# One hybrid decoder layer: the factors' reloads on GpSimd's queue, matmuls in program order, and four small moves in the order of work

## The chip, the core and the metric

The kernel runs on one core of a Trainium2 chip. The metric is the device time of one execution in microseconds; three timed runs of the kernel before took 2387.79, 2386.2 and 2385.35 us, the median is 2386.2. A core has a matrix engine (TensorE, PE in the profile, with PEld for its weight loads), three engines for elementwise work (VectorE or DVE, ScalarE or ACT, GpSimd or POOL) and a sync engine (SP) which here does nothing but issue DMAs. DMAs can also be issued from ACT's and POOL's queues.

## The reference, cut to what matters

One decoder layer for 512 tokens and a model width of 2048, everything in float32:

```python
h = rms_norm(x, g_mix)                       # 512 x 2048
aq, ak, av, rq, rk, rv, rg = split(h @ w_in) # seven parts of 1024 columns
a_out = moba_attention(rot(norm(aq)), rot(norm(ak)), av)       # 8 heads of 128, causal
r_out = silu(rg) * normed(retention(rot(rq), rot(rk), rv)) * g_ret  # 8 heads
x = x + concat(a_out, r_out) @ w_o
h2 = rms_norm(x, g_ffn)
x = x + (silu(h2 @ w_gate) * (h2 @ w_up)) @ w_down             # inner width 5632
gate = sigmoid(rms_norm(x, g_ple) @ w_ple_gate + b_ple_gate)
x = x + (p @ w_ple_proj) * gate
```

## The kernel before, in words

**Precision.** Each float32 operand is held as two reduced-precision parts, high and low. `split()` makes them: a copy on ScalarE (L54) gives the high part, a subtraction on VectorE (L55) the low one. `mm3()` then does three matmuls, high by high, high by low and low by high, all recorded at line 64, the helper `matmul()`.

**Big products.** The products with w_in's value and gate columns (w_vg), w_o, gate and up (w_gu, eleven groups), w_down (three parts of the inner width, of 8, 8 and 6 chunks of factors) and the last gate (w_pl) use a scheme of seven products in place of eight for a product of 2 x 2 blocks. A `Group` goes through its products in the order 1, 5, 6, 3, 7, 2, 4 (`ORDER`), which accumulate into three pairs of PSUM banks, X, Z and Y. The left factors of the seven products (tiles `s`) are sums and differences of activation blocks, split into high and low; the right ones are made from weight tiles `raw` as they come in: `add()` sums two blocks in place (L82), `extract()` splits the result into `wh` and `wl`, `multiply()` issues the matmuls. `run()` steps through (product, unit) pairs: in step i it extracts unit i+2, adds unit i+3 and multiplies unit i, then calls what `later()` put down for that step. `evacuate()` reads the banks when a product is done and forms the four quarters of the result, each handed to a `finish()` of its own.

**Factors on their way to the next layer part.** `finish()` of a residual or swiglu group passes results through `to_factors()` and `factors()`, which transpose, make the sums for the seven products and split them. Most of them don't fit in place: `spill()` writes them in tiles `o` and stores these to DRAM through SP's queue; `reload()` (L196 to L203) brings a whole factor tile `s` of 1 to 2 MB back, also through SP's queue, once the last matmul that reads the old tile has been issued. This happens at each passage from one layer part to the next: w_o to gate and up (from 861), gate and up to w_down (from 1700), between w_down's three parts, and w_down to the last gate (up to 2224).

**What sets the order.** A planner places instructions on each engine by priority and simulated readiness, and adds the semaphore waits. It may reorder, except where `keep_in_program_order` pins an instruction. `in_order[0]` makes `matmul()` and `transpose()` pin, and is set for the attention and retention part (about 285 to 740 us) until `take_over()` clears it. Outside that stretch the planner is free to put matmuls of the next product among those of the current one. SP's queue is one list: an instruction that waits there holds all that stand behind it.

**The start.** `beside()` loads two chunks of x transposed for each step, scales each by the norm's gain on ScalarE (L450) and splits it; the program has both scalings of a step first, then both splits. Ten idle matmuls (L396) run while the first data comes. The first matmuls are of a `Plain` projection into banks Y and Z.

**Attention, retention and p.** For each pair of heads, `projection()` multiplies h by 8 units of weights; `weights()` keeps two or three units loaded and split ahead (`ready`). The work of the pair before is placed in numbered slots among the projection's matmuls, 32 to a projection, by `tick()` and `at_slot()`. `heads()` gives the slots: for each of a pair's two heads (`plans`) when the two turnings, the four scores, the four turned weights and the result go. Scores and results share two PSUM banks, `at`. After the last projection, the product of p with its weights (pTH, then four blocks `w_pp`) is run between L896 and L913; its results go to DRAM through GpSimd's queue (L910).

**The end.** `gate()` finishes the last two groups: `finish()` multiplies by the row's scale and adds the bias (L1004), then a sigmoid on ScalarE, a product with p's tile (L1006), the residual (L82) and the store. For the last product, "4", a subtraction from the bank comes before this.

Of the kernel before, what the change touches and what calls it, by code (L numbers as in the profile page):

```python
# [10 lines left out]
F32 = mybir.dt.float32  # L11
# [22 lines left out]
def layer_kernel(ctx, tc, x, xT, pT, g_mix, wqk, w_vg, qk_norm, g_ret, w_ow, g_ffn,  # L34
# [24 lines left out]
                                           op0=ALU.mult, op1=ALU.subtract)  # L59

    in_order = [False]

    def matmul(*args, **kw):
        ins = nc.tensor.matmul(*args, **kw)  # L64
        if in_order[0]:
            tc.keep_in_program_order(ins)

    def transpose(o, a):
        ins = nc.tensor.transpose(o, a, ident)  # L69
# [126 lines left out]
    def reload(tiles, where, n, wait={}):  # L196

        def go(p):
            tiles[p] = factor_tile(p)
            nc.sync.dma_start(tiles[p][:, :n].bitcast(F32), where[p][:, :n].bitcast(F32))  # L200
            if n == 4 and p == "4":
                nc.sync.dma_start(tiles[p][:, 6:].bitcast(F32), where[p][:, 4:].bitcast(F32))
        return lambda p: later(wait[p], lambda: go(p)) if p in wait else go(p)  # L203

    class Group:
# [70 lines left out]
            for u in range(len(groups[0].units)):  # L276
                groups[0].load(q, u)

    def evacuate(finish, ahead=None):

        def evac(g, p):
            X, Y, Z = (g.bank.get(k) for k in "XYZ")
            quarter = QUARTER.get(p)
            early = [ahead(*quarter, b) if quarter and ahead else None for b in range(2)]

            def go():
                if p == "1":
                    g.e1 = [ev_tile("e1") for _ in range(2)]
                elif p == "5":
                    g.e5 = [ev_tile("e5") for _ in range(2)]  # L290
                elif p == "6":
                    g.v = [ev_tile("v") for _ in range(2)]
                for b in range(2):
                    if p == "1":
                        nc.scalar.activation(g.e1[b], X[b], AF.Copy)
                    elif p == "5":
                        nc.scalar.activation(g.e5[b], Z[b], AF.Copy)
                    elif p == "6":
                        sub(g.v[b], Y[b], g.e1[b])
                    elif p == "3":  # L300
                        plus(g.v[b], Z[b], g.v[b])
                        finish(*quarter, b, g.v[b], early[b])
                    elif p == "7":
                        sub(g.e1[b], Y[b], g.e1[b])
                        plus(g.e5[b], g.e5[b], g.e1[b])
                        finish(*quarter, b, g.e5[b], early[b])
                    elif p == "2":
                        finish(*quarter, b, X[b], early[b])
                    elif p == "4":
                        sub(g.e1[b], Y[b], g.e1[b])  # L310
                        finish(*quarter, b, g.e1[b], early[b])
            later(1 if p == "5" else 2, go)
        return evac

# [20 lines left out]
    def residual(n, i, units, old, new, turn):  # L335

        outs = {}

        def ahead(th, nh, b):
            t = ev_tile("g", 4, name="xin")  # L340
            nc.sync.dma_start(t, old(2 * th + b, 2 * n + nh))
            return t

        def finish(th, nh, b, part, t):
            tb = 2 * th + b
            s = 2 * n + nh
            o = t if (th, nh) == (0, 0) else part
            plus(o, part, t)
            later(1, lambda: nc.sync.dma_start(new(tb, s), o))
            if turn is None:  # L350
                return
            j, gain, where, tiles = turn
            sq = ev_tile("A", name="sq")
            nc.scalar.activation(sq, o, AF.Square, accum_out=ssq[j][:, tb, s:s + 1])
            outs[tb, nh] = o
            if len([k for k in outs if k[1] == nh]) < NB:
                return
            for u in range(2):
                k = 4 * n + 2 * nh + u
                sink = spill(where, k)  # L360
                if n == 1:
                    direct = into(tiles, k)
                    sink = (lambda p, a=spill(where, k - 2), b=direct: a(p) if p == "4" else b(p)) if nh else direct
                wait = 1 + 2 * u if n == 0 else units - 2 + u if nh else 1 + u
                later(wait, lambda u=u, sink=sink: to_factors(
                    lambda b: outs[b, nh], 2 * u, sink, lambda c: gain[:, 4 * s + c:4 * s + c + 1]))
            if n == 1 and nh == 0:
                rstd_of(ssq[j], rstd[j])
        return evacuate(finish, ahead)

    in_units = lambda us: [(p, u) for part in us for p in "156" for u in part] + \
# [21 lines left out]
    warm = ev_tile("v", name="warm")  # L393
    nc.scalar.activation(warm[:, :P], zeros[:, :P], AF.Copy)
    idle = tp_p.tile([P, T], F32, name="tp", tag="tp")
    for _ in range(10):  # L396
        nc.tensor.matmul(idle, zeros[:, :P], zeros, start=True, stop=True)

    class Plain:
# [90 lines left out]
    def beside(i):  # L490

        if i == 3:
            for t, c in ((ident, ident_c), (gf, g_ffn), (gp, g_ple), (gr, g_ret)):
                nc.sync.dma_start(t, c)
        if -2 <= i < NC // 2 - 2:
            if i == -2:
                first.load(0)
            chunks[i + 2] = [h_chunk(k) for k in (2 * i + 4, 2 * i + 5)]
            for c, t in enumerate(chunks[i + 2]):
                split(h[:, 2 * i + 4 + c, 0, :], h[:, 2 * i + 4 + c, 1, :], t)  # L500
            if i > -2:
                first.load(i + 2)
        if 0 <= i + 1 < NC // 2:
            first_factors(i + 1, chunks.pop(i + 1))
        for at, q in ((3, "11"), (7, "12"), (11, "22")):
            if at <= i < at + 4:
                groups[0].load(q, i - at)
        if 8 <= i < 24:
            b, s = divmod(i - 8, NS)
            t = ev_tile("o", 4, name="xn")  # L510
            tc.keep_in_program_order(nc.sync.dma_start(t, x[b * P:(b + 1) * P, s * T:(s + 1) * T]))
            nc.scalar.activation(t, t, AF.Square, accum_out=ssq[0][:, b, s:s + 1])
        elif i == 24:
            rstd_of(ssq[0], rstd[0])
# [37 lines left out]
    stream = [wqk[i, u] for i in range(1, 2 * NPAIR) for u in range(NC // 2)] + [pT] + [w_pp[n] for n in range(NS)]  # L552
    ready = []

    def weights():
        while stream and len(ready) < (3 if len(stream) > NS - 1 else 2):
            tags.append(tags.pop(0))
            raw = rawq.tile([P, 2, T], F32, name="raw", tag=tags[0])
            wh = wq.tile([P, 2, T], F32R, name="wh", tag="wh")
            wl = wq.tile([P, 2, T], F32R, name="wl", tag="wl")  # L560
            nc.sync.dma_start(raw, stream.pop(0))
            split(wh, wl, raw)
            ready.append((wh, wl))
        return ready.pop(0)

    def projection(rows):

        accs = [acc_p.tile([P, T], F32, name="acc", tag="acc") for _ in range(4)]
        for u in range(NC // 2):
            wh, wl = weights()  # L570
            for f in range(4):
                tick()
                at = slice(f * P, (f + 1) * P)
                for c in range(2):
                    k = 2 * u + c
                    H, L = hT[k]
                    if rows:
                        mm3(accs[f], H[:, at], L[:, at], wh[:, c, :], wl[:, c, :], k == 0, k == NC - 1)
                    else:
                        mm3(accs[f], wh[:, c, at], wl[:, c, at], H, L, k == 0, k == NC - 1)  # L580
        return accs

    sides = ap.tile([P, 3, P], F32, name="sides", tag="dec")
# [268 lines left out]
    def heads(i, made):  # L852
# [7 lines left out]
        if i < NPAIR:  # L860
            plans = ((12, (15, 16, 19, 20), (19, 20, 23, 24), 27), (21, (25, 26, 39, 40), (29, 30, 42, 43), 46))
            if i == 0:
                plans = ((17, (20, 21, 24, 25), (24, 25, 28, 29), 33), (26, (30, 31, 39, 40), (38, 39, 43, 44), 47))
            for j, (turns, steps_s, steps_w, last) in enumerate(plans):
                turned, scores, weights_turned, result = attend(*made, v, j)
                put(turned, turns, turns + 1)
# [116 lines left out]
                                         (2, gp, s_h3, s_e) if kg == 2 else None), None, after))  # L983

    bias_t = []

    def load_bias():
        for s in range(NS):
# [4 lines left out]
    def gate(n):  # L993
        def ahead(th, nh, b):
            tb, s = 2 * th + b, 2 * n + nh
            t = [ev_tile("g", 4, name="xin"), ev_tile("g", 4, name="pp")]
            nc.sync.dma_start(t[0], xd[3][tb][:, s])
            nc.sync.dma_start(t[1], ppd[tb][:, s])
            return t

        def finish(th, nh, b, part, t):
            tb, s = 2 * th + b, 2 * n + nh
            o = ev_tile("A", name="y") if (th, nh) == (0, 0) else part
            nc.vector.scalar_tensor_tensor(o, part, rstd[2][:, tb:tb + 1], bias_t[s], op0=ALU.mult, op1=ALU.add)  # L1004
            nc.scalar.activation(o, o, AF.Sigmoid)
            nc.vector.tensor_tensor(o, o, t[1], op=ALU.mult)  # L1006
            plus(o, o, t[0])
            nc.sync.dma_start(out[tb * P:(tb + 1) * P, s * T:(s + 1) * T], o)
        return evacuate(finish, ahead)

    for n in range(2):
        groups.append(Group(lambda kh, nh, u, n=n: w_pl[n, kh, nh, u], range(4), s_e, gate(n),
# [81 lines left out]
```

## Time and profile before

| what | value |
|---|---|
| timed runs, us | 2387.79, 2386.2, 2385.35 (median 2386.2) |
| the profiled execution, its own time | 2389.06 us |
| its span | 2387.3 us |
| busy: PE, PEld, DVE, ACT, POOL | 97%, 80%, 81%, 50%, 2% |
| matmuls | 10470 |
| mean granted TensorE clock | 0.993 of full speed |
| DMA traffic | 463.60 MB, mean 194 GB/s |
| the chain that ended last | PE 79%, DVE 12%, DMA 5% |

The span lies between the first and the last instruction of the profiled execution; the time of that execution is 1.8 us longer. A busy share is the part of the span in which an engine had an instruction under way. Matmuls are pipelined: one of 512 columns shows as 0.39 to 0.50 us, and the next starts about 0.23 us after it.

### The profile page before, as it was taken

Reading aid. Unit: us, or ns where it says so; the run is one execution under the profiler, and the core shown is the slowest. Engines: PE = TensorE matmul, PEld = TensorE weight load, DVE = VectorE, ACT = ScalarE, POOL = GpSimd, SP = SyncE. Lnnn points to the kernel's source line nnn. Section 1 sums busy time; section 2 is a strip of 40 time slices with the busy share of each in tenths; the row PEclk is TensorE's granted clock in tenths of the full one; section 3 lists DMA queues with packets and bytes.
Section 4 is the critical chain, followed back from the end, with each engine's and each line's share of the span. In section 5 each row is a group of like instructions: output and inputs, shape, how many; then the busy total and the mean of one; then the engine's idle time right before and its main releaser. Section 6 shows DMA issues by size and latency. Waiting matters only on the chain.

```text
span 2387.3 us, 29151 instructions
## 1 busy us (share of the span) xinstructions
PE 2323.2 (97%) x10470; PEld 1901.7 (80%) x10470; DVE 1944.3 (81%) x2625; ACT 1204.9 (50%) x1791; POOL 48.2 (2%) x47
## 2 busy tenths in 40 slices
PE   9999999999999999999999999999999999999898
PEld 7888877778877777888888888888878878888677
DVE  8888676666667988888988898889888878789897
ACT  7644444444455565545554455455544433356543
POOL 0000021100010000000000000000000000000000
PEclk9999999999999999999999999999999999999999
DMA  6634733446666684356435643464587666867664
GB/s 230 240 129 161 233 102 119 128 139 189 188 217 257 227 311 162 122 177 187 143 117 167 198 142 126 143 199 153 198 341 232 253 242 220 324 222 249 253 203 124
DMA packets 166098, 463.60 MB, mean 194 GB/s; under 512 B 18497, under 2 KB 31169, under 8 KB 160961
## 3 DMA queue, kind: packets, MB, share of 16 engines
q1 hardware_dynamic: 161968, 453.34, 56.0%
q10 hardware_dynamic: 2704, 4.20, 0.7%
q0 software_dynamic: 1280, 4.20, 0.5%
q8 instruction: 82, 1.34, 0.2%
q14 instruction: 64, 0.52, 0.1%
HBM read 352.09 MB, written 105.38 MB: 192 GB/s over the span
## 4 chain that ended last, share of the span: by engine, by line
PE 79%; DVE 12%; DMA 5%; issue 2%; ACT 2%; POOL 0%; SPq 0%; ACTq 0%; DVEq 0%; POOLq 0%
PE Y L64 29%; PE Z L64 19%; PE X L64 17%; PE acc L64 9%; DVE wl L55 3%; DVE raw L82 3%; PE at L64 2%; DMA h<-o 2%; PE tp L69 2%; ACT wh L54 1%; DMA mix<-o 1%; DVE s L55 1%; DVE t L79 1%; DVE o L55 0%; DVE e L79 0%
## 5 line engine op out<-in xcount | busy, mean ns | idle before, releaser
L54 ACT ACTIVATE wh<-raw 128x1024 fp32r<-128x1024 f32 (+1 forms) x728 | 769.1, 1059 | 827.6 <-PE Y L64 289.2
L55 DVE TENSOR_TENSOR wl<-raw,wh 128x1024 fp32r<-128x1024 f32 (+1 forms) x728 | 883.1, 1218 | 277.2 <-ACT wh L54 276.3
L64 PE MATMUL Y<-wh,s 128*128 128x512 f32 x2160 | 680.8, 391 | 9.7 <-ACT wh L54 9.7
L64 PEld LDWEIGHTS Y<-wh,s 128*128 128x128 f32 x2160 | 405.3, 188 | 97.2 <-ACT wh L54 14.1
L64 PE MATMUL Z<-wh,s 128*128 128x512 f32 x1504 | 476.0, 392 | 2.6 <-DMA s<-h 1.6
L82 DVE TENSOR_TENSOR raw<-raw 128x1024 f32<-128x1024 f32 x376 | 453.0, 1217 | 27.4 <-DMA raw<-in_w_gu 9.6
L64 PE MATMUL Y<-wl,s 128*128 128x512 f32 x1080 | 425.1, 394 | 1.4 <-DVE wl L55 1.3
L64 PE MATMUL X<-wh,s 128*128 128x512 f32 x1312 | 416.9, 393 | 8.0 <-ACT wh L54 5.1
L64 PEld LDWEIGHTS Z<-wh,s 128*128 128x128 f32 x1504 | 282.1, 188 | 62.0 <-ACT wh L54 2.8
L64 PE MATMUL Z<-wl,s 128*128 128x512 f32 x752 | 297.1, 395 | 4.6 <-DVE wl L55 4.5
L64 PEld LDWEIGHTS X<-wh,s 128*128 128x128 f32 x1312 | 247.3, 189 | 62.1 <-ACT wh L54 7.8
L64 PE MATMUL X<-wl,s 128*128 128x512 f32 x656 | 258.7, 394 | 4.9 <-DVE wl L55 4.7
L64 PEld LDWEIGHTS Y<-wl,s 128*128 128x128 f32 x1080 | 203.2, 188 | 45.6 <-DVE wl L55 4.3
L64 PEld LDWEIGHTS Z<-wl,s 128*128 128x128 f32 x752 | 141.6, 188 | 37.9 <-DVE wl L55 9.3
L64 PE MATMUL acc<-h,wh 128*128 128x512 f32 x512 | 160.4, 394 | 0.8 <-DVE m L666 0.8
L64 PEld LDWEIGHTS X<-wl,s 128*128 128x128 f32 x656 | 124.1, 189 | 34.0 <-DVE wl L55 8.4
L64 PE MATMUL acc<-wh,h 128*128 128x512 f32 x384 | 130.8, 400 | 1.5 <-DVE m L666 1.1
L64 PEld LDWEIGHTS acc<-h,wh 128*128 128x128 f32 x512 | 92.5, 188 | 17.5 <-issue 1.2
L64 PE MATMUL acc<-h,wl 128*128 128x512 f32 x256 | 100.1, 391 | 0.0
L64 PEld LDWEIGHTS acc<-wh,h 128*128 128x128 f32 x384 | 72.9, 190 | 17.0 <-issue 2.7
L64 PE MATMUL acc<-wl,h 128*128 128x512 f32 x192 | 75.6, 394 | 0.0
L79 DVE TENSOR_TENSOR e<-Y,e 128x512 f32<-128x512 f32 x96 | 62.8, 682 | 14.5 <-PE Y L64 14.5
(193 smaller groups left out, 2069.7 us busy)
## 6 DMA issues: line engine op xcount, KB each, us to landing
raw<-in_w_gu SPq DMA_DIRECT2D x176, 512.0 KB, 4.3
raw<-in_w_dn SPq DMA_DIRECT2D x88, 512.0 KB, 6.1
a<-o SPq DMA_DIRECT2D x154, 256.0 KB, 2.6
raw<-in_wqk SPq DMA_DIRECT2D x63, 512.0 KB, 3.8
s<-a SPq DMA_DIRECT2D x14, 2048.0 KB, 10.8
raw<-in_w_vg SPq DMA_DIRECT2D x48, 512.0 KB, 5.2
raw<-in_w_ow SPq DMA_DIRECT2D x32, 512.0 KB, 6.1
xin<-x SPq DMA_DIRECT2D x64, 256.0 KB, 6.0
```

The costliest lines, as they stand in the source:

```text
L54: nc.scalar.activation(H, src, AF.Copy)
L55: nc.vector.tensor_tensor(L, src, H.bitcast(F32), op=ALU.subtract)
L64: ins = nc.tensor.matmul(*args, **kw)
L69: ins = nc.tensor.transpose(o, a, ident)
L79: nc.vector.tensor_tensor(o, a, b, op=ALU.subtract)
L82: nc.vector.tensor_tensor(o, a, b, op=ALU.add)
```

## The change

All reloads of factors are issued from GpSimd's queue. Every matmul that isn't pinned gets a dependency without a semaphore on the matmul before it in the program, so that the planner keeps their order; transposes are not in that chain. `weights()` is cut into `fill(n)` and the pop; after the last of its units, a projection with fewer than four units left in the stream calls `fill(3)`. In the first pair's plan the first head's result goes from slot 33 to 32 and the second head's second score from 31 to 33. At the start each chunk is scaled and split before the next is loaded, and 13 idle matmuls take the place of 10. For the last gate, `minus` holds the negated row scale; when product "7" is done, `ready()` turns the partial sum into bias minus scale times it, and product "4" then needs a single instruction from the bank in place of a subtraction and a scale-and-add.

```diff
+    last_mm = [None]
     def matmul(*args, **kw):
         ins = nc.tensor.matmul(*args, **kw)
         if in_order[0]:
             tc.keep_in_program_order(ins)
+        elif last_mm[0] is not None:
+            tc.add_manual_dep(ins.ins, last_mm[0], mybir.DependencyInfo(mybir.DependencyClass.NoSync, mybir.DependencyReason.DATA),
+                              reason="matmuls in program order")
+        last_mm[0] = ins.ins.name
...
         def go(p):
             tiles[p] = factor_tile(p)
-            nc.sync.dma_start(tiles[p][:, :n].bitcast(F32), where[p][:, :n].bitcast(F32))
+            nc.gpsimd.dma_start(tiles[p][:, :n].bitcast(F32), where[p][:, :n].bitcast(F32))
             if n == 4 and p == "4":
-                nc.sync.dma_start(tiles[p][:, 6:].bitcast(F32), where[p][:, 4:].bitcast(F32))
+                nc.gpsimd.dma_start(tiles[p][:, 6:].bitcast(F32), where[p][:, 4:].bitcast(F32))
...
                         finish(*quarter, b, g.e5[b], early[b])
+                        if ready is not None:
+                            ready(*QUARTER["4"], b, g.e1[b])
...
                     elif p == "4":
-                        sub(g.e1[b], Y[b], g.e1[b])
-                        finish(*quarter, b, g.e1[b], early[b])
+                        if ready is None:
+                            sub(g.e1[b], Y[b], g.e1[b])
+                        finish(*quarter, b, g.e1[b], early[b], *([Y[b]] if ready else []))
...
                 rstd_of(ssq[j], rstd[j])
+                if j == 2:
+                    nc.vector.tensor_scalar(minus, rstd[j], -1.0, None, op0=ALU.mult)
...
-    for _ in range(10):
+    for _ in range(13):
...
-            chunks[i + 2] = [h_chunk(k) for k in (2 * i + 4, 2 * i + 5)]
-            for c, t in enumerate(chunks[i + 2]):
-                split(h[:, 2 * i + 4 + c, 0, :], h[:, 2 * i + 4 + c, 1, :], t)
+            chunks[i + 2] = []
+            for k in (2 * i + 4, 2 * i + 5):
+                t = h_chunk(k)
+                split(h[:, k, 0, :], h[:, k, 1, :], t)
+                chunks[i + 2].append(t)
...
-    def weights():
-        while stream and len(ready) < (3 if len(stream) > NS - 1 else 2):
+    def fill(n):
+        while stream and len(ready) < n:
...
+    def weights():
+        fill(3 if len(stream) > NS - 1 else 2)
         return ready.pop(0)
...
+        if len(stream) < NS:
+            fill(3)
         return accs
...
-                plans = ((17, (20, 21, 24, 25), (24, 25, 28, 29), 33), (26, (30, 31, 39, 40), (38, 39, 43, 44), 47))
+                plans = ((17, (20, 21, 24, 25), (24, 25, 28, 29), 32), (26, (30, 33, 39, 40), (38, 39, 43, 44), 47))
...
+    minus = stat.tile([P, NB], F32, name="minus", bufs=1)
...
+        def ready(th, nh, b, w):
+            tb, s = 2 * th + b, 2 * n + nh
+            nc.vector.scalar_tensor_tensor(w, w, minus[:, tb:tb + 1], bias_t[s], op0=ALU.mult, op1=ALU.add)
+
-        def finish(th, nh, b, part, t):
+        def finish(th, nh, b, part, t, bank=None):
             tb, s = 2 * th + b, 2 * n + nh
             o = ev_tile("A", name="y") if (th, nh) == (0, 0) else part
-            nc.vector.scalar_tensor_tensor(o, part, rstd[2][:, tb:tb + 1], bias_t[s], op0=ALU.mult, op1=ALU.add)
+            nc.vector.scalar_tensor_tensor(o, part if bank is None else bank, rstd[2][:, tb:tb + 1],
+                                           bias_t[s] if bank is None else part, op0=ALU.mult, op1=ALU.add)
```

## Rows read from the trace of the kernel before

**Rows 1.** The page, busy time of each engine over the span.
```profile
PE 2323.2 (97%) x10470; PEld 1901.7 (80%) x10470; DVE 1944.3 (81%) x2625; ACT 1204.9 (50%) x1791; POOL 48.2 (2%) x47
```

**Rows 2.** Busy by stretch: length, PE, PEld, DVE, ACT, POOL, clock, DMA share, GB/s.
```profile
690.17:705.65 15.48, 11.80 (x51) 9.11 (x50) 15.47 (x26) 11.28 (x22) 4.53 (x8) 1.00 0.81 262
868.00:893.00 25.00, 23.36 (x109) 18.79 (x108) 19.94 (x36) 16.84 (x34) 0.00 (x0) 1.00 0.93 349
893.00:940.00 47.00, 39.64 (x159) 29.90 (x158) 41.53 (x58) 25.59 (x44) 1.01 (x1) 0.89 0.42 169
940.00:1740.00 800.00, 800.00 (x3603) 661.28 (x3603) 687.04 (x814) 408.20 (x528) 0.00 (x0) 1.00 0.51 163
1740.00:1785.00 45.00, 40.59 (x182) 32.34 (x181) 33.70 (x41) 19.41 (x26) 0.00 (x0) 1.00 0.89 361
1920.00:1940.00 20.00, 17.61 (x71) 14.07 (x70) 14.71 (x15) 5.76 (x6) 0.00 (x0) 0.91 1.02 417
2150.00:2245.00 95.00, 89.23 (x403) 70.81 (x403) 93.33 (x144) 62.09 (x116) 1.11 (x1) 1.00 0.80 285
2245.00:2256.00 11.00, 8.90 (x24) 6.47 (x23) 6.87 (x10) 4.67 (x7) 0.00 (x0) 0.70 0.18 50
```

**Rows 3.** The same view, stretches at the lower clock (columns as in rows 2).
```profile
9.07:12.48 3.41, 3.41 (x10) 2.65 (x9) 3.41 (x9) 3.41 (x9) 0.00 (x0) 0.50 1.05 408
343.58:346.99 3.41, 3.41 (x13) 2.93 (x12) 3.41 (x8) 1.01 (x2) 0.57 (x1) 0.50 0.00 0
896.54:906.77 10.23, 7.50 (x21) 5.21 (x22) 8.62 (x20) 9.40 (x20) 1.01 (x1) 0.50 1.03 415
```

**Rows 4.** Waits of SP's queue, 855 to 912: total us, times, longest.
```profile
SPq L200 <- DMA h<-o: 7.9, 2, 5.2
```

**Rows 5.** Waits of ScalarE, 855 to 905: total us, times, longest.
```profile
ACT o L54 <- DMA h<-o: 10.6, 2, 6.3
```

**Rows 6.** Timeline at the start: start, duration, instruction, [idle before <- releaser].
```profile
6.83 0.72 ACT L450 ACTIVATE x<-x,gm 128x512 f32<-128x512 f32 x1 [0.22 <-DMA x<-in_xT]
7.46 0.61 ACT L54 ACTIVATE h<-x 128x512 fp32r<-128x512 f32 x1
...
8.12 0.50 PE L64 MATMUL Y<-wh,h 128*128 128x512 f32 x1 [2.45 <-ACT h L54]
```

**Rows 7.** Timeline of TensorE, two pairs of matmuls that go first.
```profile
225.81 0.74 PE L64 MATMUL Y<-wh,s 128*128 128x512 f32 x2 [0.74 <-ACT wh L54]
...
993.73 0.71 PE L64 MATMUL Z<-wh,s 128*128 128x512 f32 x2
```

**Rows 8.** Timeline of VectorE just before the second of them.
```profile
990.83 1.22 DVE L55 TENSOR_TENSOR wl<-raw,wh 128x1024 fp32r<-128x1024 f32 x1
```

**Rows 9.** Timeline of TensorE, the first pair's result.
```profile
342.20 0.50 PE L64 MATMUL at<-PH,v 128*128 128x512 f32 x1 [2.12 <-ACT pt L719]
```

**Rows 10.** Timeline of TensorE, the waits at p's product.
```profile
696.27 0.50 PE L64 MATMUL acc<-wl,wh 128*128 128x512 f32 x1 [2.33 <-DVE wl L55]
...
703.36 0.50 PE L64 MATMUL acc<-wl,wh 128*128 128x512 f32 x1 [1.34 <-DVE wl L55]
```

**Rows 11.** The reloads' line L200: issue ns (min/median/max), landing us.
```profile
L200 SPq DMA_DIRECT2D s<-a x21: 319/326/383, 1700.0 to 2085.6; - x21
L200 SPq DMA_DIRECT2D s<-h x14: 319/320/468, 861.0 to 2224.0; - x14
...
DMA to landing us min/median/max: 5.3/9.9/13.4
```

**Rows 12.** GpSimd's stores of p, line L910: issue ns, landing us.
```profile
L910 POOL DMA_DIRECT2D pp<-pp x16: 539/540/731, 691.8 to 725.7; - x16
...
DMA to landing us min/median/max: 2.7/6.9/8.8
```

**Rows 13.** Timeline of VectorE, first and last instruction after the last matmul.
```profile
2378.18 0.69 DVE L79 TENSOR_TENSOR e<-Y,e 128x512 f32<-128x512 f32 x1 [2.96 <-PE Y L64]
...
2383.01 0.69 DVE L82 TENSOR_TENSOR e<-e,xin 128x512 f32<-128x512 f32 x1
```

More of the change, by code (lines that the diff above doesn't have):

```diff
@@ L277, in chained, with evacuate @@
                 groups[0].load(q, u)
-    def evacuate(finish, ahead=None):
+    def evacuate(finish, ahead=None, ready=None):
         def evac(g, p):
@@ L1008, in finish @@
             nc.sync.dma_start(out[tb * P:(tb + 1) * P, s * T:(s + 1) * T], o)
-        return evacuate(finish, ahead)
+        return evacuate(finish, ahead, ready)
     for n in range(2):
```

## The prediction

> **What bounds the kernel now.** The page comes first: TensorE is busy for 97% of the span, VectorE for 81%, ScalarE for half [rows 1]. A busy TensorE is therefore the ground, and only time in which it stands idle, or runs at the lower clock, can be won. The table by stretch says where that is [rows 2]. In the eleven gate-and-up groups, from 940 to 1740, PE is busy for 800.00 of 800 us: nothing is to be had there. Idle time sits where one layer part passes into the next: 868 to 940 (1.6 + 7.4 us), 1740 to 1785 (4.4), 1920 to 1940 (2.4) and 2150 to 2256 (5.8 + 2.1). In three of the four the DMA engines are full for most of the time, and in the first and last VectorE is close to full as well. Then the clock: after such idle time the granted clock falls to 0.5, the lower level of 1.2 GHz, and PE works on at half speed [rows 3]; short rows like the first two stand also at 1930.8, 2244.8 and 2251.6 (3.4 us each), and half of such a stretch's busy time is lost. The waits of the SP queue and of ScalarE tell why data is late at a passage [rows 4, 5]: the reloads of the factors (L200) stand in SP's queue until a spill store has landed, 7.9 us around 861 to 870, and everything behind them stands too, weights included; ScalarE waits 10.6 us for stores from the spill buffers that left late.
>
> **The edits, each with its sum.** The sum is made on the profiled execution, which took 2389.06 us with a span of 2387.3; that is 2.9 above the median of the three timed runs, 2386.2, from which I subtract.
>
> *Start (L396, L498).* The second chunk's scaling holds ScalarE at 6.83, after 0.22 us of waiting for its DMA, and the first split follows only at 7.46; the first matmul waits for that until 8.12 [rows 6]. Split behind scaling lets the split go at 6.61, 0.85 sooner. Three more idle matmuls (L396) cost nothing, since PE is idle then anyway for 2.45 us. If the shorter pause keeps the clock up, the half-speed row from 9.07 loses nothing, 3.41 / 2 = 1.7 more. Against that, matmuls in program order want the second chunk's low part at the fifth matmul, where now twelve others go first; three steps of the kind of that 0.61 us split lie before it, so I estimate it some 2 us late for that. From -1 to 2.6; I take 0.9.
>
> *Program order for unpinned matmuls (L63).* Now two matmuls of the next product often stand ahead of the last ten, or last 22, of the one before. There are 69 such pairs outside the pinned stretch. Five of them (at 147, 224, 825, 1866 and 2025) pull the next product's weights forward to before ScalarE has split them, and cost 0.74 us of idle and 0.9 us of pitch each, as at 225.81 [rows 7]; the matmuls passed over were ready. 5 x 0.9 = 4.5. The other pairs fill no hole: at 993.73 the pair goes first, yet the low weights of the product it overtakes were done at 990.83 + 1.22 = 992.05 [rows 7, 8]. From 0 to 6; I take 4.5.
>
> *First pair's result a slot earlier (L863).* The result's matmul waits 2.12 us at 342.20 for the exponential of a score from three slots before, since the two `at` banks are both with scores; then the clock falls, and 343.58 to 346.99 goes at half speed, 1.7 us lost [rows 3, 9]. In the new plan the result takes the free bank first, and the second score comes two slots later. It then waits for that same exponential, but two thirds of the time has been filled with the result. 3.8 less a new wait of some 0.8 is 3.0; from 0 to 3.8.
>
> *p's second weights (L555, L581).* PE waits 2.33 us at 696.27 and 1.34 at 703.36, both times for low weights from VectorE [rows 10]. The fill at the end of the last projection brings the first of the two splits ahead of the rotary work, so the first wait goes. But VectorE is busy for 15.47 of the 15.48 us from 690 to 705.6 [rows 2], and what is late next is the third block's split at its end: it moves up only by the one subtraction (1.2 us) that left the queue. So 1.2, from 0 to 3.7.
>
> *Reloads on GpSimd's queue (L200, L202).* Thirty-five reloads of 1 to 2 MB and two small ones leave SP; each issue cost SP 0.32 us and landed after 9.9 in the median [rows 11]. What changes is what stands behind them: weights, residual tiles and spill stores no longer wait at SP for a spill store's landing. The four passages hold 9.0, 4.4, 2.4 and 7.9 us of idle [rows 2]. The clock adds 2.5 in the first (half of the matmul part of the row from 896.54 [rows 3]), 1.7 in the third, 3.4 in the last. Together 31.3 us, the most that can come. How much of it comes I read from VectorE's share: where it has time (the second and third passage, 33.70 of 45 and 14.71 of 20) I take three quarters of 4.4 + 4.1, 6.4; in the first (61.5 of 72) half of 11.5, 5.7; in the last, where VectorE is busy for 93.33 of 95 and PE waits mainly for its work, a third of 11.3, 3.8. That makes 15.9. On the other side, a GpSimd issue takes 0.54 us, and its 256 KB stores landed after 6.9 in the median, on full queues [rows 12]; 35 x 0.54 = 19 us would be lost if every one were waited for. They stand far ahead of use, and GpSimd is busy for 2%, so I take none. GpSimd's only other work behind them is the norm's power, two instructions of 1 us [rows 2] whose results are wanted tens of us later. Ends: -19 and 31.
>
> The Trainium skill (SBUF — State Buffer, section "SBUF: two separate sides") warns that a DMA issued from GpSimd needs descriptors that GpSimd must write, and that some VectorE instructions lock it out meanwhile. The trace agrees only so far as it goes: with VectorE full from 690 to 705.6 [rows 2], the sixteen issues took 0.54 us each and at most 0.73 [rows 12]. By the page the reloads could come late at any full stretch; by the row they do not.
>
> *The gate's bias (L1010, L1001).* After the last matmul VectorE runs eight instructions back to back, from 2378.18 to 2383.70. Two are subtractions, of the kind of the one at 2378.18 (0.69 each, [rows 13]), which move to an earlier product as a scalar_tensor_tensor each, in place of the subtraction there; VectorE has gaps at that point. Of 1.4 us the second bank's own end keeps a part: 0.8, from 0.7 to 1.4.
>
> *What comes back.* The order on ScalarE and VectorE is planned anew when queues and matmuls change. Rows show what one misplaced weight costs: 1.34 and 2.33 at p [rows 10], 2.4 in 1920 to 1940 [rows 2]. I allow three new ones, 6 us.
>
> Sum: 0.9 + 4.5 + 3.0 + 1.2 + 15.9 + 0.8 - 6 = 20.3. **2366 us**.
>
> **The rivals.** *The DMA engines were the limit.* At 893 to 907 and 1920 to 1940 they are full (1.03 and 1.02 at 415 GB/s and more [rows 2, 3]); the same bytes on two queues come no sooner, and a late weight stays late. Then the 15.9 fall away, and half of what comes back: 20.3 - 15.9 + 3 = 7, 2379. For it: in three of the four they are at 80% or more [rows 2]. Against: at 868 to 893 the engines have 7% to spare while SP stands, and a weight wanted now is worth more than a factor wanted 30 us later. The Trainium skill (DMA: Bandwidth & Descriptors, section "Issuing engines are not separate DMA queues") says that a second issuing engine saves only the issue's own time; by that rule this rival is right, but SP's waits [rows 4] are not issue time, so the trace bears it out only in part.
>
> *All of it comes.* The passages close wholly and no new wait appears: 31.3 + 0.9 + 4.5 + 3.0 + 1.2 + 0.8 = 41.7, 2345. Against: VectorE has 1.7 us free in 2150 to 2245.
>
> *Late reloads.* Each of the five sets' first reload comes 5 us late behind GpSimd's descriptors, because both queues now share the engines, and PE waits: 25 us lost instead of the 15.9 won, nothing else new: 0.9 + 4.5 + 3.0 + 1.2 + 0.8 - 25 = -15, 2401. It decides from the point where a reload lands after its product's first matmul is due.
>
> *The overtaking pairs were needed.* If the low weights come later than the pair covers, each of the 69 places waits 0.45 us: 31 us lost, 2366 + 31 + 4.5 = 2401. The row at 990.83 [rows 8] speaks against it with 1.2 us to spare; where VectorE is full (11 pairs in 2150 to 2245) it could hold.
>
> **Chances.** Forecast 0.52; DMA the limit 0.20; all of it 0.08; late reloads 0.10; pairs needed 0.10, mixed with smaller gains. A difference of under 0.2% (4.8 us) is not told from none. Faster: 0.52 + 0.08 + 0.15 of the DMA rival = 0.75; within: 0.05 + 0.07 of the two losing ones = 0.12; slower 0.13. The range goes from 2349, near the whole, to 2387, which takes in the DMA rival and leaves out the losses; the forecast's own is 2356 to 2378.
>
> **What would show it.** L200 on POOL, SP's waits for spill stores gone between 855 and 905, PE busy for over 66 of the 72 us around the first passage; no `Y` pair inside a run of `Z` at 225; no half-speed row at 343; the first wait at p gone and the second grown; six instructions after the last matmul instead of eight. Wrong would be: idle PE of the same size at the passages with raw landings as late as before, a PE wait on a reload at each passage, or 0.4 us waits on low weights all through 940 to 1740.

## The result and the profile after

The changed kernel took 2406.6 us in the median against 2387.2 for the kernel before: a ratio of 1.0075, interval 1.0056 to 1.0093. The change makes the kernel slower by 19 us, where 2366 had been forecast. The profiled execution took 2406.24 us; the working below is on its span, 2404.4 against 2387.3, a difference of 17.1.

On the page TensorE's share is still 97% [rows 1], and GpSimd now moves 60 MB where it moved 4.20 before. The page after, busy times and the two large DMA queues (packets, MB, share of 16 engines):

```profile
PE 2331.8 (97%) x10473; PEld 1909.7 (79%) x10473; DVE 1944.2 (81%) x2626; ACT 1207.8 (50%) x1791; POOL 66.4 (3%) x84
...
q1 hardware_dynamic: 156640, 397.24, 49.9%
q0 software_dynamic: 6608, 60.30, 6.4%
```

To see where 17 us came from I set the n-th matmul of one trace beside the n-th of the other, without the three more idle matmuls at the start, and cut both at the same matmuls (the order of some matmuls differs, which makes this uncertain by some 0.5 us). Lengths against the kernel before, in us, for the stretches that begin and end at these times of its trace; beside the start, stretches in which no row reaches 2 are left out:

| kernel | 0-60 | 285-345 | 345-690 | 690-740 | 868-940 | 1740-1785 | 1920-1945 | 2080-2110 | 2150-2256 | span |
|---|---|---|---|---|---|---|---|---|---|---|
| after | +0.4 | -3.0 | +3.3 | +3.1 | +4.3 | +3.9 | +3.8 | +5.2 | -2.4 | +17.1 |
| reloads on SP | +0.3 | -3.0 | +1.8 | +2.1 | -2.5 | +0.4 | 0.0 | +0.5 | +0.6 | +2.0 |
| reloads on GpSimd alone | -0.1 | +0.7 | -0.7 | -0.2 | +4.5 | +2.5 | +1.6 | +5.2 | +2.3 | +15.6 |

So 17.2 us are lost in four of the five passages of factors, and 3.1 at p; what the small edits win elsewhere is given back. Rows 2 again in the trace after, each stretch cut at the same matmuls (length, PE, PEld, DVE, ACT, POOL, clock, DMA share, GB/s):

```profile
871.00:896.00 25.00, 24.20 (x115) 19.84 (x113) 21.30 (x39) 16.15 (x33) 2.17 (x4) 1.00 1.02 401
896.00:947.20 51.20, 40.16 (x150) 30.57 (x151) 39.01 (x53) 24.19 (x40) 2.17 (x3) 0.83 0.33 129
947.20:1747.80 800.60, 800.60 (x3604) 661.34 (x3603) 687.41 (x815) 408.19 (x529) 2.12 (x4) 1.00 0.51 163
1747.80:1796.70 48.90, 43.50 (x182) 34.39 (x181) 35.55 (x42) 20.30 (x28) 1.60 (x3) 0.93 0.80 331
```

The eleven gate-and-up groups are full as before. At the passages PE stands idle longer (11.0 us in the second row against 7.4 of [rows 2]) and more of the time is at the lower clock: a mean of 0.83 against 0.89, and 0.93 in the fourth row where it had been 1.00. The longest wait at the first passage, in the timeline of TensorE after, and under it the instruction of ScalarE that it waited for:

```profile
903.09 0.79 PE L65 MATMUL X<-wh,s 128*128 128x512 f32 x1 [5.80 <-ACT wh L54]
```

```profile
901.98 1.06 ACT L54 ACTIVATE wh<-raw 128x1024 fp32r<-128x1024 f32 x1 [7.94 <-DMA raw<-in_w_gu]
```

The first matmul of the new layer part waits for split weights, and the split for a weight load, not for a reloaded factor: the profile after names no engine that waited for the reloads' line. That load left SP at 887.7 and landed 14.2 us later. Three reloads of 1 MB had left GpSimd just before it, at 883.8, 884.6 and 886.0. In the kernel before they left at 886.4, 888.9 and 891.7, and the trace after runs 3 us late at this place; so off SP's queue they went out some 6 to 9 us sooner.

How weights become late is seen in the DMA view of 30 us at the passage to w_down, at the same place of both kernels. Before, one queue carries everything:

```profile
q1 hardware_dynamic: 2750, 12.39, 101.1%
...
s<-a SPq DMA_DIRECT2D x3, 2048.0 KB, 12.2
raw<-in_w_dn SPq DMA_DIRECT2D x9, 512.0 KB, 10.4
```

After:

```profile
q1 hardware_dynamic: 2400, 6.98, 57.8%
q0 software_dynamic: 388, 5.57, 43.5%
...
s<-a POOLq DMA_DIRECT2D x3, 2048.0 KB, 10.9
raw<-in_w_dn SPq DMA_DIRECT2D x8, 512.0 KB, 12.9
```

The engines are full in both and move the same 12.4 to 12.6 MB. But now they serve the two queues side by side, nearly half and half, and a reload lands 1.3 us sooner and a weight tile 2.5 us later. The weights are wanted within some us, the factors of a product only when the next group comes to it, six products later.

### The profile page after: what moved, and what is told of

The parts are those of the page before. It is cut to its first block, busy times and chain, and to the rows that moved or that the text cites. A ratio compares the mean times of both kernels' runs of the same rounds, so it can differ in the third digit from the quotient of the medians.

```text
span 2404.4 us, 29226 instructions
## 1 busy us (share of the span) xinstructions
PE 2331.8 (97%) x10473; PEld 1909.7 (79%) x10473; DVE 1944.2 (81%) x2626; ACT 1207.8 (50%) x1791; POOL 66.4 (3%) x84
## 3 DMA queue, kind: packets, MB, share of 16 engines
q8 instruction: 82, 1.34, 0.2%
## 4 chain that ended last, share of the span: by engine, by line
PE 76%; DVE 13%; DMA 6%; issue 3%; ACT 2%; SPq 0%; POOL 0%; ACTq 0%; DVEq 0%
PE Y L65 28%; PE Z L65 18%; PE X L65 16%; PE acc L65 10%; DVE wl L55 4%; DVE raw L87 4%; PE at L65 2%; DMA raw<-in_w_dn 2%; PE tp L74 2%; ACT wh L54 1%; DMA h<-o 1%; DMA raw<-in_w_gu 1%; DMA mix<-o 1%; DMA pp<-pp 0%; DVE m L684 0%
## 5 line engine op out<-in xcount | busy, mean ns | idle before, releaser
L65 PE MATMUL X<-wh,s 128*128 128x512 f32 x1312 | 423.8, 398 | 17.3 <-ACT wh L54 13.9
L65 PEld LDWEIGHTS X<-wh,s 128*128 128x128 f32 x1312 | 252.4, 192 | 72.2 <-ACT wh L54 15.8
L65 PE MATMUL X<-wl,s 128*128 128x512 f32 x656 | 263.7, 402 | 9.1 <-DVE wl L55 9.1
L84 DVE TENSOR_TENSOR e<-Y,e 128x512 f32<-128x512 f32 x92 | 60.3, 684 | 11.9 <-PE Y L65 11.9
```

Of the source, the lines that this page charges most:

```text
L84: nc.vector.tensor_tensor(o, a, b, op=ALU.subtract)
```

## The experiments

Two theories stood against each other at first. A: the second queue takes engines from SP's transfers when these are full. B: with the matmuls in program order, TensorE can't fill a hole at a passage with matmuls of the next product. Later came D: GpSimd's way of issuing is what costs. (C, in one expectation, is that the elementwise engines are late by themselves.)

**Reloads back on SP, all else changed.**

```diff
-            nc.gpsimd.dma_start(tiles[p][:, :n]...)
+            nc.sync.dma_start(tiles[p][:, :n]...)
```

> The changed kernel (2406.6 us) with the reloads of the factors back on SP's queue; all else as changed. Theory A (shared engines): at the passages the sixteen DMA engines are full, and reloads from a second queue take half of them away from SP's weights, residual tiles and spill stores, which TensorE waits for first; this costs nearly all of the loss, so the time comes to 2384 to 2391, the 5.8 us wait of an X matmul for split weights at 897 goes, and no SP transfer of 0.25 to 0.5 MB takes over 13 us to land at 880 to 910. Theory B (program order of the matmuls: TensorE can no longer put matmuls of the next product into a hole): 2400 or more, with the X matmuls' waits at 897, 1785 and 1938 still there.

2389.57 us, ratio 0.9999 (0.9990 to 1.0008): no change against the kernel before, and 17 us less than the changed kernel. The 5.8 us wait is gone; the passages are back (table above). A holds, B falls.

**Without the dependency between matmuls, reloads on GpSimd.**

```diff
-        elif last_mm[0] is not None:
-            tc.add_manual_dep(ins.ins, last_mm[0], ...)
```

> The changed kernel without the dependency between unpinned matmuls; reloads stay on GpSimd's queue. Theory A: 2400 to 2409, the waits at the passages stay. Theory B: 2392 or less, pairs of matmuls of the next product go into the holes again.

2405.16 us, 1.0066 (1.0053 to 1.0079). The loss stays: +4.2, +2.0, +1.3, +4.0 and +2.7 in the last five stretches of the table.

**The kernel before with only the reloads moved.**

> The kernel before (2387.2 us) with one edit, the reloads on GpSimd's queue. Theory A: 2400 to 2408, slower by 13 to 20, lost at 868 to 940, 1740 to 1790, 1920 to 1960 and 2090 to 2260. Theory B: 2389 or less.

2405.06 us, 1.0068 (1.0054 to 1.0083): this one edit is the loss. In its trace the sixteen weight loads around the passage to w_down show the pattern singly: compared with the kernel before, and with the 4.65 us by which the trace runs late taken off, those issued at 1738.8, 1741.4 or 1743.7 land some 1 to 4 us later, and the reload issued at 1744.5 lands 3.2 us sooner. Landing of these sixteen loads, before and in this kernel (us, min/median/max):

```profile
DMA to landing us min/median/max: 5.3/10.0/12.4
```

```profile
DMA to landing us min/median/max: 4.1/11.9/16.9
```

**Both undone: the small edits alone.**

> The changed kernel with reloads on SP's queue and without the dependency between matmuls: only the start, the first pair's slot, p's weights and the gate's bias are left of the change. Theory A and B: 2384 to 2391. By theory A it stands within 3 us of the kernel that has the dependency as well; by theory B it is 10 us or more faster than that one. The stretch 690 to 740 should end 3 us later relative to the first matmul than in the kernel before, as in the changed kernel (two falls of the clock).

2389.81 us, 1.0008 (0.9999 to 1.0016). So start, first pair, p and bias together move nothing measurable, and the program order adds 0 to that (2389.57 with it). From 690 to 740 this version loses 2.1 us, where 3 had been expected.

**A delay that did not take hold.** The reload's call was put 10 to 14 group steps later in the program, with the tile taken at once, on SP in the kernel before and on GpSimd in the changed one; then on SP with all small edits, and the same without the fill of p's weights.

```diff
-            tiles[p] = factor_tile(p)
-            nc.sync.dma_start(...)
+        def take(p):
+            tiles[p] = factor_tile(p)
+            later(wait.get(p, 0), lambda: go(p))
```

> The kernel before (2387.2 us, reloads on SP's queue) with one edit: the tile is taken at once as now, but the reload's DMA is issued later in program order, by 14 of the group steps of 2.7 us (10 for w_down's third part, 12 for products 3, 7, 2 and 4 at the two turnings), into the stretch behind each passage in which the DMA engines stand nearly idle. If full DMA engines at the passages are what makes weights and residual tiles late (theory A), the passages' idle time shrinks: 2370 to 2382. If the time is lost to the order of engines' work and not to transfers (theory C: VectorE and ScalarE are what is late there), no gain: 2385 to 2391. If a delayed reload becomes late itself, 2392 or more, with PE waiting for s.

> The changed kernel (2406.6 us), reloads still on GpSimd's queue, each issued later by the same steps. Theory A (the second queue's bytes take the engines from SP's at the wrong time): most of the loss comes back, 2375 to 2392. Theory D (it is GpSimd's way of issuing that costs, whenever it happens): 2400 to 2408.

> The changed kernel with reloads on SP's queue and later by the same steps: the small edits and the program order on top of the delay. By theory A within 4 us of the kernel before with the delay alone, since the small edits together moved nothing measurable (0.9999 to 1.0008): 2368 to 2384.

> The same without the early fill of p's second weights. The traces with the fill show two falls of the clock at 702 and 722, worth 3.4 us, against 2.4 us of waiting saved at p; without it the time should be 1 to 4 us less than with it, and the clock should stay at full speed from 690 to 740. If the fill does no harm: within 1 us.

2389.73 us (1.0006, 0.9997 to 1.0014), 2404.8 (1.0062, 1.0050 to 1.0074), 2387.57 (0.9996, 0.9987 to 1.0004) and 2386.2 (0.9991, 0.9982 to 0.9999). All these expectations of a gain missed, but they tell nothing of A: the first reload of w_down still went out at 1697.8 in the first of them against 1700.0 before, and at 1709.9 in the second against 1708.4 after. A later place of the call in the program did not make it a later DMA. For the fill: without it 1.4 us less, with overlapping intervals. The clock stayed at full speed from 690 to 740, but in this pair it did so with the fill too, so the two falls remain unexplained.

**Reloads on GpSimd, held by a semaphore.** Now each reload waits for the last matmul of 14 steps later (10 and 12 as before).

```diff
+            tc.add_manual_dep(one.ins, last_mm[0],
+                mybir.DependencyInfo(mybir.DependencyClass.Sync, mybir.DependencyReason.DATA), reason="paced")
```

> The changed kernel (2406.6 us), reloads on GpSimd's queue, each held by a semaphore until the last matmul of 14 group steps later has run (10 and 12 steps as in the earlier delay). The earlier delay did not take hold: the first seven reloads of w_down were issued at 1710 to 1777 with it and at 1708 to 1775 without. Theory A (the second queue takes half of full DMA engines from weights that are wanted sooner): with the reloads moved into the stretch behind the passage, 2380 to 2396. Theory D (issuing from GpSimd costs whenever it happens): 2400 to 2409. If a held reload is late itself: PE waits for s, 2405 or more.

2384.28 us, 0.9983 (0.9973 to 0.9994): some 22 us less than the changed kernel (timed in other rounds), by the reloads' time alone. The reloads' line in this trace, and under it the landing of the same sixteen weight loads:

```profile
L204 POOL DMA_DIRECT2D s<-a x21: 527/527/539, 1735.7 to 2112.9; - x21
L204 POOL DMA_DIRECT2D s<-h x14: 527/534/606, 862.2 to 2253.1; - x14
```

```profile
DMA to landing us min/median/max: 3.6/6.4/12.8
```

It issues as long from GpSimd (0.53 us) as the changed kernel does, and nobody waits for that. D falls. Two queues side by side are not enough for a loss either: from 1736 to 1766 the reloads have 47.5% of the engines here and SP's queue 52.8%, much as in the changed kernel. What differs is the run-up. In the 40 us from 1700 to 1740, cut at the same matmuls, four reloads go out in the kernel before and after, one in this version; spill stores issued there land after 8.3, 7.8 and 3.1 us in the median. No run separates late weights from late spill stores.

**Reloads on SP, behind the weights.** Same delays, no fill; in place of the semaphore an order in SP's queue.

```diff
+            tc.add_manual_dep(one.ins, last_load[0],
+                mybir.DependencyInfo(mybir.DependencyClass.NoSync, mybir.DependencyReason.DATA), reason="behind the weights")
...
+            last_load[0] = ins.ins.name     # in Group.load
```

> The version without the early fill and with the reloads on SP (2386.2 us with the delay that did not take hold), each reload now ordered in SP's queue behind the last weight load that the program has issued 14 (10, 12) group steps later, without a semaphore. The first reload of w_down then stands behind 144 weight loads in place of 140. Theory A: weights come sooner at the passages, 2372 to 2383. If the full engines are the limit whatever the order: 2384 to 2390.

2372.23 us, 0.9928 (0.9916 to 0.9941): faster than both kernels. The stretch that was 1740 to 1785 takes 39.8 us instead of 45 and has no idle PE, with the DMA engines as full as ever:

```profile
1733.70:1773.50 39.80, 39.80 (x183) 32.84 (x182) 30.59 (x32) 19.46 (x23) 0.00 (x0) 1.00 1.01 413
```

Its seven reloads around there, on SP, and their landing; then the landing of the sixteen weight loads:

```profile
L205 SPq DMA_DIRECT2D s<-a x7: 319/320/689, 1733.4 to 1792.4; - x7
...
DMA to landing us min/median/max: 10.4/14.2/23.1
```

```profile
DMA to landing us min/median/max: 3.4/6.4/13.1
```

Reloads may take up to 23 us here and no matmul waits for one.

**The same order in the kernel before, none of the change's edits.**

> The kernel before (2387.2 us) with one edit: the reloads stay on SP's queue, but each is ordered behind the weight loads of 14 (10, 12) group steps later, as in the fastest version (2372.2 us); none of the change's own edits. If the order of reloads and weights at the passages is the whole gain (theory A): 2371 to 2378. If the small edits or the program order of the matmuls carry part of it: 2379 to 2386.

2375.82 us, 0.9947 (0.9935 to 0.9959), the same sixteen loads at 6.3 in the median. So 13 of the 17 us come from the order alone. The other 3.6 between the two medians would be the small edits and the program order together, without the fill; the intervals overlap a little, so I leave that unproven.

**Reloads on ScalarE's queue.**

```diff
-            nc.sync.dma_start(tiles[p][:, :n]...)
+            nc.scalar.dma_start(tiles[p][:, :n]...)
```

> The kernel before with the reloads on ScalarE's queue, which like SP's is served without descriptors from GpSimd. Theory A: any second queue takes its half; weights issued before a reload land some 4 us later than in the kernel before, 2398 to 2412 (with whatever ScalarE loses by waiting at the head of its queue). Theory D: only GpSimd's way of issuing costs, 2386 to 2394.

2419.53 us, 1.0127 (1.0113 to 1.0141). The time is above A's range, and A's other sign missed: the sixteen weight loads landed sooner than before (9.0 in the median), not 4 us later. So this run doesn't bear out that any second queue makes weights late, and since ScalarE itself is disturbed in it, it doesn't refute that. PE stood 5.0 us for a weight's low part in 1700 to 1790. ScalarE waited longer than before for free weight tiles (in the kernel before the same waits from 1692 to 1792 are 10.3 us with 1.7 the longest, and 4.0 with 1.7); its waits from 1700 to 1800 in this trace (us in total, times, longest):

```profile
ACT wh L54 <- PE X L64: 12.3, 7, 3.9
ACT wh L54 <- PE Z L64: 11.0, 5, 5.7
```

I read it as reloads at the head of ScalarE's queue that hold the splits behind them; that was not tested.

How late the weights land and how long the passage takes, in seven kernels (landing: median of the sixteen loads; length: the stretch 1740 to 1785, which is 45 before):

| kernel | landing | length |
|---|---|---|
| reloads on GpSimd alone | 11.9 | 47.5 |
| after | 11.5 | 48.9 |
| before | 10.0 | 45.0 |
| reloads on SP, all else changed | 9.6 | 45.4 |
| on GpSimd, held | 6.4 | 40.2 |
| on SP, behind the weights | 6.4 | 39.8 |
| the same in the kernel before | 6.3 | 39.7 |

Early weights, at 6.3 to 6.4, go with a passage of some 40 us. Among the later ones there is no order: the seven other kernels have 9.0 to 12.9 us with 45.1 to 48.3, and the small edits alone, with reloads on SP, have 9.4 with 48.0. So 1740 to 1785 doesn't tell the queues apart. Three other stretches do. Against the kernel before, the four kernels whose reloads go out on GpSimd as soon as they can lose 3.5 to 4.5 us from 868 to 940, 1.3 to 4.0 from 1920 to 1945 and 4.0 to 5.2 from 2080 to 2110. The five with the change's other edits or the delay that did not take hold and reloads on SP have -5.2 to -0.3, 0.0 to 0.1 and -0.4 to 0.5 there.

## Why the prediction was wrong, step by step

**Reloads on GpSimd's queue: the step that failed.** The prediction counted 15.9 us won because "weights, residual tiles and spill stores no longer wait at SP". Measured alone it costs 16.5 (2405.06 against 2388.6 for the kernel before, timed beside it), and 17.0 on top of the other edits (2406.6 against 2389.57, timed in different rounds). The waits for spill stores at SP did shrink, but nothing was won by it. From 855 to 912 SP's waits for spill stores fell from 14.3 to 4.0 us, and its waits for weight loads to land grew from 6.6 to 12.0. Idle PE at the passages with late weights was the first sign of being wrong that the prediction named. The largest of the waits for weight loads after:

```profile
SPq L222 <- DMA raw<-in_w_gu: 6.9, 4, 2.4
```

Two things were wrong in the step. The queue was not what limited the transfers: [rows 2] shows engines at 0.93, 0.89 and 1.02 in three of the passages and 0.80 in the fourth, so a queue for the reloads alone mostly changes who is served. And it changes it the wrong way. In one queue a 2 MB reload stood behind the weights issued before it: in the kernel before, weights issued at 1740.5, 1742.0 and 1745.3 land before the reload issued at 1746.6. With the reloads on GpSimd alone, the reload issued at 1744.5 (4.65 us taken off, as above) lands before the two weight tiles issued 0.8 and 3.1 us ahead of it. At the first passage the second queue also let three reloads out some 6 to 9 us sooner, just ahead of the load that TensorE then waited for. The Trainium skill bears on this (DMA: Bandwidth & Descriptors, section "Issuing engines are not separate DMA queues"): DMAs of all issuers run on the same sixteen engines and interleave, and a second issuer saves only issue time. The traces bear out the interleaving, and the runs show that saved issue time is not the whole price: moving the reloads cost 16.5 us.

**The rivals.** "The DMA engines were the limit" had the cause, but its price was 0 for the reloads, since it took the order of the bytes to be indifferent. "Late reloads" came within 6 us of the time by luck: not the reloads landed late (9.6 us in the median of all, as 9.9 before [rows 11]), but what shared the engines with them. "The overtaking pairs were needed" falls as a cause of the loss: 947 to 1748 is as full as before, and without the dependency nothing is won.

**GpSimd's issue.** Costed at nothing; that holds. The reloads' line after:

```profile
L205 POOL DMA_DIRECT2D s<-a x21: 530/530/542, 1708.4 to 2101.4; - x21
L205 POOL DMA_DIRECT2D s<-h x14: 530/540/606, 864.8 to 2245.1; - x14
```

No issue took over 0.61 us, and the reloads landed as soon as before. The trap of the Trainium skill (SBUF — State Buffer, section "SBUF: two separate sides") did not show here. That page ties it to VectorE instructions in a two-port mode; whether any ran beside an issue no view here tells.

**Start.** 0.9 forecast; 0.4 lost, within what the comparison can tell from none. The first split moved only from 7.46 to 7.32: the planner puts the second scaling first again, as the trace after shows ScalarE doing:

```profile
6.70 0.72 ACT L461 ACTIVATE x<-x,gm 128x512 f32<-128x512 f32 x1 [0.44 <-DMA x<-in_xT]
7.32 0.62 ACT L54 ACTIVATE h<-x 128x512 fp32r<-128x512 f32 x1
```

The stretch at the lower clock from 9.07 stayed (0.51 after). In four other traces with the same start it is missing, and 0.4 to 2.1 us are won from 0 to 60. It is missing too in one with the old start (the first delay, on SP), so it does not hang on this edit alone.

**Program order.** 4.5 forecast. The waits on high weights of [rows 7] are gone, but the low part is late next, 0.43 us in place of 0.74 at the same place after:

```profile
224.93 0.50 PE L65 MATMUL Z<-wl,s 128*128 128x512 f32 x1 [0.43 <-DVE wl L55]
```

That leaves 0.3 us at this place. Over the whole kernel nothing is measurable (2389.57 with, 2389.81 without), and two traces say why. With the reloads on SP, and for banks X, Y and Z, the dependency takes TensorE's waits for high weights from 14.4 to 6.2 us and its waits for low weights from 10.0 to 27.1. The largest of these, without and with the dependency (us in total, times, longest):

```profile
PE Z L65 <- DVE wl L55: 4.6, 7, 2.1
```

```profile
PE Z L65 <- DVE wl L55: 12.8, 19, 2.3
```

So the step's "The other pairs fill no hole" does not hold as far as these two traces show: without the pairs low weights are late at 33 places against 16, as the rival had it, though not at its 69.

**First pair's result.** 3.0 forecast; 3.0 are won from 285 to 345, where the wait of [rows 9] is gone, and lost again from 345 to 690 (+3.3). The new wait that I had put at 0.8 is another one, a transpose that waits 2.15 for VectorE, and in this trace a fall of the clock stands beside it (350.3 to 353.7 at 0.51). The fall isn't all of it: with the reloads on SP the clock stays at 1.00 from 340 to 360, and 1.8 us are still lost from 345 to 690. The wait in the timeline, and the stretches at the lower clock, after:

```profile
350.43 0.47 PE L74 MATMUL tp<-ident,pt 128*128 128x128 f32 x1 [2.15 <-DVE pt L739]
```

```profile
350.30:353.70 3.40, 3.27 (x10) 2.55 (x11) 0.91 (x5) 1.41 (x5) 0.74 (x1) 0.51 0.78 282
701.90:705.30 3.40, 3.40 (x9) 2.65 (x9) 3.21 (x5) 1.75 (x3) 0.55 (x1) 0.50 1.02 412
722.40:729.20 6.80, 5.55 (x14) 4.58 (x15) 4.78 (x9) 2.82 (x7) 1.58 (x2) 0.50 1.04 368
899.90:910.10 10.20, 6.28 (x14) 4.19 (x14) 4.30 (x6) 2.78 (x6) 1.57 (x2) 0.50 1.03 413
```

**p's second weights.** 1.2 won forecast, 3.1 lost in this trace. As the prediction had it, the first wait goes and the second grows; what it missed is w_o's first product, which waits for a bank that ScalarE empties too late, and a fall of the clock beside each of the two long waits (rows above). TensorE after:

```profile
701.62 0.56 PE L65 MATMUL acc<-wl,wh 128*128 128x512 f32 x1 [2.66 <-DVE wl L55]
718.82 0.50 PE L65 MATMUL X<-wh,s 128*128 128x512 f32 x1 [0.23 <-ACT pp L927]
723.65 0.79 PE L65 MATMUL X<-wh,s 128*128 128x512 f32 x1 [3.18 <-ACT pp L927]
```

The waits sum to 6.1 us, against 6.4 before (2.33 and 1.34 of [rows 10], and 0.96 and 1.80 at the bank). The falls are not the fill's doing alone: one trace with it has none between 690 and 740, and the fastest version's, without it, has two.

**The gate's bias.** 0.8 forecast; 1.0 found, as 8.0 us lie between the last matmul's end and the span's end before and 7.0 after, with six instructions on VectorE instead of eight. This step was right in the trace; a gain of that size can't be told in the timed runs.

**New waits.** 6 us were allowed for a new plan of ScalarE and VectorE. The waits for low weights under "Program order" are of that kind: 17.1 us more of them, against 8.2 less for high weights.

## What to carry to other kernels

Before moving a transfer to a second queue, look at the DMA share of the stretch: where the engines are full, as here, a queue is an order of service, and a second one lets bulk that is wanted late overtake what is wanted now. Put such bulk behind the urgent transfers in the same queue, or hold it until the stretch behind. And when a planner places instructions, check in the trace that a moved call moved.

## What was not expected of the hardware

Two queues with work shared full engines close to evenly (57.8% and 43.5% over 30 us, 52.8% and 47.5% over 30 us in the version with held reloads), although one packet of the reloads carried about 14 KB and one of SP's about 3 KB in that window (5.57 MB / 388, 6.98 MB / 2400).
